# An eighth block by seven products, ordinary units placed by phase, and a weight sum made by an accumulating DMA

## The chip, the core and the metric

The kernel runs on one core of one Trainium2 chip. The metric is the device time of one execution in microseconds (us). The core's engines are named as in the profile: PE (TensorE's matmuls), PEld (its weight loads), DVE (VectorE), ACT (ScalarE), POOL (GpSimd) and SP (SyncE, which only issues DMAs here).

## The reference

Two layers work on x of 256 tokens by 2048 columns, in float32:

```
h  = RMSNorm(x);  z = h @ w_in                    # 2048 x 3584
A  = chunked spatial gating of gelu(z[:, :2048])  # 2 chunks of 128 tokens
B  = sliding-window attention with sinks on the rest of z
x += concat(RMSNorm(A), RMSNorm(B)) @ w_out       # 2048 x 2048
h2 = RMSNorm(x)
x += (silu(h2 @ w_gate) * (h2 @ w_up)) @ w_down   # 2048 x 5632, twice, and 5632 x 2048
```

Three quarters of the matmul work lies in the last line, the feed-forward part (FFN below), and the change is there.

## The kernel before

**Split products.** Each float32 product is made of three matmuls. `split2` makes two tiles of a raw weight tile (128 x 2 x 512): ACT casts it to `wh` (L95) and DVE subtracts to get the rest, `wl` (L96). `mm3` (L125 to L127) multiplies the activation's high part with `wh` and `wl`, and its low part with `wh`. Raw weights come by SP's DMA queue (`raw_load`) into a ring of six tiles, `wh` and `wl` have rings of four.

**Ordinary units.** `unit` takes one raw tile and does 12 matmuls with 512 columns: two halves of the tile, two blocks of 128 tokens, three matmuls each. A block of 512 FFN columns takes 8 units for the gate and 8 for up (`gate_up`, through `even`), then Silu and product (L656, L660). `down` multiplies one or two finished blocks by `w_down`, four column blocks of 512 after one another, and DVE adds each result to the residual `xres` (L680). Both write to a pair of PSUM banks called `dacc` while the other stream is running, and to `acc` afterwards.

**Blocks by seven products.** `seven` treats gate and up weights and the two token blocks as a 2 x 2 by 2 x 2 block product and gets it with 7 products in place of 8. It needs sums of the activations (`ext`, made once per layer in `combine`) and sums of the weights, made by DVE for each block. Its `s_unit` splits one tile and does 6 matmuls. **Phase A** has four products, 16 s_units in four groups: b11 (m0 in the matmuls' tile names), t1 = b11 + b12 (m1), t2 = t1 + b22 (m3) and b12 + b22 (m2). Three weight sums of 128 x 1024 go with each group (L594 to L596). At the middle, ACT and DVE combine the banks into `m1`, `u1`, `c21` and `c22` (L605 to L612). **Phase B** has three products, 12 s_units: b21 (n0), t2 + b21 (n1) and b22 (n2). The fourth sum (L621) is in this phase; the four t2 tiles are kept for it. At the end DVE and ACT make `sg` (L628 to L632), and `act_T` transposes it on PE (`ps_f`) and splits it (L560, L561), as it does after a `gate_up`.

**Order.** The work is written out by a planner. `tick` moves a clock by 1 per ordinary unit and by 0.5 per s_unit, and `later` puts off a step by so many units: `act_T` comes 2 and 3 units after its block. In the FFN the list `S_BLOCKS` is the stream of blocks by seven products, and `STD_ORDER` the other stream: four gate_ups (blocks 0, 2, 4, 6) and the down products of all eleven blocks. After each s_unit the loop at L695 adds 0.5 x `STD_SHARE` to what it owes to the other stream, and emits as many ordinary units as are due; at a turn (the middle and the end of a seven-block) it owes at least 2. The other stream yields False, and emits nothing, while a down waits for the `act_T` of one of its blocks. A scheduler then orders the instructions within a short distance.

The loop before:

```python
for said in s_stream():
    owed = max(owed, 2.0) if said == "turn" else owed + said * STD_SHARE
    while owed >= 1.0 and next(other, False):
        owed -= 1.0
```

Of the kernel before, what the change touches and what calls it, by code (L numbers as in the profile page):

```python
# [12 lines left out]
F32 = mybir.dt.float32  # L13
F32R = mybir.dt.float32r
BF16 = mybir.dt.bfloat16
AF = mybir.ActivationFunctionType
ALU = mybir.AluOpType
# [4 lines left out]
P = 128  # L22
# [4 lines left out]
HD = 64  # L27
NH = 16
NKV = 4
GRP = NH // NKV  # L30
# [5 lines left out]
NB = 512  # L36
# [3 lines left out]
NI = 3584 // NB  # L40
NFF = DFF // NB
ND = D // NB
S_BLOCKS = (1, 3, 5, 7, 8, 9, 10)
STD_ORDER = (
    ("gu", 0), ("gu", 2), ("down", (0, 1)), ("gu", 4), ("down", (2, 3)), ("gu", 6),
    ("down", (4, 5)), ("down", (6, 7)), ("down", (8, 9)), ("down", (10,)),
)
STD_SHARE = 1.42
RL = 512
WARM = 12  # L50

# [12 lines left out]
def trunk(ctx, tc, x, xt, w_in, w_out, w_gate, w_up, w_down, sgu_w, sgu_g, consts,  # L64
          rel_bias, onehot, radd, out):
    nc = tc.nc

    cp = ctx.enter_context(tc.tile_pool(name="cp", bufs=1))
    wp = ctx.enter_context(tc.tile_pool(name="wp", bufs=1))
    tp = ctx.enter_context(tc.tile_pool(name="tp", bufs=8))  # L70
    zp = ctx.enter_context(tc.tile_pool(name="zp", bufs=8))
    ap = ctx.enter_context(tc.tile_pool(name="ap", bufs=2))
# [7 lines left out]
        return t.bitcast(F32)  # L80

    def raw_load(src, parts=1):
        raw = wp.tile([P, 2, NB], F32, tag="raw", name="raw", bufs=6)
        n = 2 // parts
        for i in range(parts):
            nc.sync.dma_start(raw[:, i * n : (i + 1) * n, :], src[:, i * n : (i + 1) * n, :])
        return raw
# [32 lines left out]
    def small_ps(shape, name):  # L120
        pool, tag = ((pm, "sm"), (pd, "dacc"))[next(turns) % 2]
        return pool.tile(shape, F32, tag=tag, name=name)
# [25 lines left out]

    cst = cp.tile([P, L, C_L], F32, tag="cst", name="cst")
    nc.sync.dma_start(cst, consts)  # L150
    junk = cp.tile([P, NB], BF16, tag="junk", name="junk")
    nc.vector.memset(junk, 1.0)
    heat = small_ps([P, NB], "heat")
    for i in range(WARM):
# [8 lines left out]
    def small(shape, name):  # L163
        return sp.tile(shape, F32, tag=name, name=name)
# [27 lines left out]
        return ps  # L192

    def sum_sq(dst, src):
        nc.scalar.activation(junk[:, : src.free_size()], src, AF.Square, accum_out=dst)

    def finish_rms(ss, width):
        tot = small([P, 1], "tot")
# [57 lines left out]
    for lay in range(L):  # L256
# [62 lines left out]
        ob = {}  # L319
# [8 lines left out]
        def attend(g, t, par, zkv=zkv, kT=kT, qT=qT, ob=ob, bias=bias, layer=layer):  # L328
            nk = (t + 1) * P
            k0 = SEQ - nk  # L330
            nh = 2 * len(par)
            heads = [h for h in range(GRP) if h % 2 in par]
            step = heads[1] - heads[0]
            nkb = nk // P
            nsink = layer["nsink"]
            s = ap.tile([P, nh, nk], F32, tag="spt", name="s", bufs=4)
            for r in par:
                ps = small_ps([P, 2, nk], "ps_s")
                for i in range(2):
                    h = g * GRP + 2 * i + r  # L340
                    nc.tensor.matmul(
                        ps[:, i, :],
                        qT[h // 8][HD * r : HD * r + HD, (h % 8) // 2, t * P : (t + 1) * P],
                        kT[HD * r : HD * r + HD, g, :nk],
                        start=True,
                        stop=True,
                    )
                nc.vector.scalar_tensor_tensor(
                    s[:, par.index(r) :: len(par), :], ps, 1.0 / math.sqrt(HD),
                    bias[g][:, r::2, k0:], ALU.mult, ALU.add,  # L350
                )
            m = small([P, nh], f"m{nh}")
            nc.vector.tensor_reduce(m, s, AX.X, ALU.max)
            hs = slice(g * GRP + heads[0], (g + 1) * GRP, step)
            nm = small([P, nh], f"nm{nh}")
            nc.vector.scalar_tensor_tensor(nm, m, -1.0, nsink[:, hs], ALU.mult, ALU.min)
            es = small([P, nh], f"es{nh}")
            nc.vector.tensor_tensor(es, nm, nsink[:, hs], ALU.subtract)
            den = small([P, nh], f"den{nh}")
            for i in range(nh):  # L360
                nc.scalar.activation(
                    s[:, i, :], s[:, i, :], AF.Exp, bias=nm[:, i : i + 1],
                    accum_out=den[:, i : i + 1],
                )
            nc.scalar.activation(es, es, AF.Exp)
            rden = small([P, nh], f"rden{nh}")
            nc.vector.tensor_tensor(rden, den, es, ALU.add)
            nc.vector.reciprocal(rden, rden)
            pt = ap.tile([P, nh * nkb, P], F32, tag="spt", name="pt", bufs=4)

            def turn():
                pst = small_ps([P, nh * nkb, P], "ps_p")
                s4 = s.rearrange("p h (b k) -> p (h b) k", k=P)
                for i in range(nh * nkb):
                    nc.tensor.transpose(pst[:, i, :], s4[:, i, :], ident)
                nc.vector.tensor_copy(pt, pst)

            def weigh():
                pv = small_ps([P, nh, HD], "ps_v")
                for i in range(nh):  # L380
                    for b in range(nkb):
                        nc.tensor.matmul(  # L382
                            pv[:, i, :],
                            pt[:, i * nkb + b, :],
                            zkv[b][:, (NKV + g) * HD : (NKV + g + 1) * HD],
                            start=b == 0,
                            stop=b == nkb - 1,
                        )
                if (g, t) not in ob:
                    ob[g, t] = ap.tile([P, GRP * HD], F32, tag=f"ob{t}", name="ob", bufs=1)  # L390
                o3 = ob[g, t].rearrange("p (h d) -> p h d", d=HD)
                nc.vector.tensor_tensor(o3[:, heads[0] :: step, :], pv, bc(rden, HD), ALU.mult)

            later(3, turn)
            later(5, weigh)
# [172 lines left out]
        def seven(b, lay=lay, pairs2=pairs2, ext2=ext2, act_later=act_later):  # L568
            bank = [pa.tile([P, NB], F32, tag="acc", name=f"m{i}") for i in range(4)]

            def s_unit(raw, m, i, op, first, last):
                wh, wl = split2(raw)
                for j in range(2):
                    ah, al = (op(2 * i + j, h) for h in range(2))
                    mm3(bank[m], ah, al, wh[:, j, :], wl[:, j, :], first and j == 0, last and j == 1)
                tick(0.5)

            def a_op(k, t):
                return lambda p, h: pairs2[p][:, h, k, t * P : (t + 1) * P]

            def e_op(n):
                return lambda p, h: ext2[p][:, h, n, :]

            kept = []
            for i in range(4):
                b12 = raw_load(w_up[lay, b, i, 0])
                b11 = raw_load(w_gate[lay, b, i, 0])
                b22 = raw_load(w_up[lay, b, i, 1])
                t1 = wp.tile([P, 2, NB], F32, tag="raw", name="t1", bufs=6)
                t2 = ap.tile([P, 2, NB], F32, tag="spt", name="t2", bufs=4)  # L590
                first, last = i == 0, i == 3
                s_unit(b11, 0, i, a_op(0, 0), first, last)
                yield 0.5
                nc.vector.tensor_tensor(t1, b11, b12, ALU.add)  # L594
                nc.vector.tensor_tensor(t2, t1, b22, ALU.add)
                nc.vector.tensor_tensor(b12, b12, b22, ALU.add)  # L596
                s_unit(t1, 1, i, e_op(1), first, last)
                yield 0.5
                s_unit(t2, 3, i, e_op(2), first, last)
                yield 0.5  # L600
                s_unit(b12, 2, i, e_op(0), first, last)
                yield 0.5
                kept.append(t2)
            m1 = zp.tile([P, NB], F32, tag="z", name="m1")
            nc.scalar.copy(m1, bank[0])  # L605
# [9 lines left out]
            for i in range(4):  # L615
                b21 = raw_load(w_gate[lay, b, i, 1])
                b22 = raw_load(w_up[lay, b, i, 1])
                first, last = i == 0, i == 3
                s_unit(b21, 0, i, a_op(1, 0), first, last)
                yield 0.5  # L620
                nc.vector.tensor_tensor(kept[i], kept[i], b21, ALU.add)  # L621
                s_unit(kept[i], 1, i, a_op(1, 1), first, last)
                yield 0.5
                s_unit(b22, 2, i, e_op(3), first, last)
                yield 0.5
            sg = [m1, c21]
            for t, m in ((0, m1), (1, c21)):
                nc.vector.tensor_tensor(m, bank[t], m, ALU.add)  # L628
# [9 lines left out]
        def s_stream(seven=seven):  # L638
            for b in S_BLOCKS:
                yield from seven(b)  # L640
# [52 lines left out]
        other = std_stream()  # L693
        owed = 0.0
        for said in s_stream():  # L695
            owed = max(owed, 2.0) if said == "turn" else owed + said * STD_SHARE
            while owed >= 1.0 and next(other, False):
                owed -= 1.0
        seven_done[0] = True
        for went in other:  # L700
            if not went:
# [89 lines left out]
```

## Time and profile before

| | us |
|---|---|
| median of 3 runs (lowest, highest) | 2028.45 (2026.97, 2030.02) |
| profiled execution | 2025.57 |
| its span, first to last instruction | 2023.9 |
| first matmul of a seven-block, layer 0 and layer 1 | 299.9 and 1305.5 |
| last matmul of a seven-block, layer 0 and layer 1 | 986.4 and 1991.1 |
| granted TensorE clock, mean | 0.994 |

In the profile a row names engine, line, operation and tiles as out<-in, with buffer numbers left out. Busy time is the union of an engine's instructions. A matmul's duration is modelled and longer than the distance between two starts, so for PE and for an engine without gaps the starts are what is read. A window row gives busy time and instruction counts of each engine in one stretch, then the granted clock, the share of the 16 DMA engines, and GB/s.

### The profile page before, as it was taken

What the parts mean: (1) busy time and instruction counts of PE and PEld (TensorE: products, weight loads), DVE (VectorE), ACT (ScalarE), POOL (GpSimd) and SP (SyncE); (2) the same over time, 40 slices, a digit from 0 to 9 for tenths busy, and PEclk for the clock granted to TensorE, in tenths of its full rate; (3) what the DMA queues carried; (4) which work ended last, traced back from release to release, by engine and by line L of the source; (5) the groups of instructions that cost most, each with busy time, mean ns of one, the idle gap of its engine ahead of it and who ended that gap; (6) DMA issues with size and microseconds to landing.
All of it is one profiled execution on the core that took longest, in us unless ns stands there. A gap on an engine that the chain in (4) does not pass through costs nothing.

```text
span 2023.9 us, 24694 instructions
## 1 busy us (share of the span) xinstructions
PE 1984.0 (98%) x8990; PEld 1618.5 (80%) x8990; DVE 1666.0 (82%) x1925; ACT 1132.3 (56%) x1415; POOL 67.5 (3%) x65
## 2 busy tenths in 40 slices
PE   8999999999999999999899999999999999999997
PEld 6878888888888888877687788888888888888776
DVE  5767689898989898997867776898989898989976
ACT  6455566555555555554654655666555555555543
POOL 1211000000000000000002100000000000000000
PEclk9999999999999999999999999999999999999999
DMA  9643556565766576665555344565656565657653
GB/s 323 226 162 134 187 178 227 201 235 194 238 209 234 201 236 212 234 204 193 198 188 192 131 156 179 175 233 203 239 206 234 202 239 202 233 204 241 215 186 137
DMA packets 117401, 416.02 MB, mean 206 GB/s; under 512 B 12912, under 2 KB 15088, under 8 KB 117280
## 3 DMA queue, kind: packets, MB, share of 16 engines
q1 hardware_dynamic: 115136, 407.01, 58.4%
q0 software_dynamic: 2144, 7.44, 1.2%
q8 instruction: 70, 1.15, 0.2%
q14 instruction: 51, 0.42, 0.1%
HBM read 412.27 MB, written 4.23 MB: 206 GB/s over the span
## 4 chain that ended last, share of the span: by engine, by line
PE 85%; DVE 9%; issue 2%; DMA 1%; ACT 1%; POOL 1%; SPq 0%; POOLq 0%; ACTq 0%; DVEq 0%
PE dacc L125 12%; PE dacc L126 12%; PE dacc L127 12%; PE acc L126 8%; PE acc L125 8%; PE acc L127 8%; DVE wl L96 4%; PE m L126 4%; PE m L127 4%; PE m L125 4%; PE n L126 3%; PE n L127 3%; PE n L125 3%; PE ps_v L382 1%; DMA raw<-in_w_gate_dram 1%
## 5 line engine op out<-in xcount | busy, mean ns | idle before, releaser
L95 ACT CAST wh<-raw 128x1024 fp32r<-128x1024 f32 (+1 forms) x706 | 739.5, 1050 | 593.2 <-PE dacc L127 293.2
L96 DVE TENSOR_TENSOR wl<-raw,wh 128x1024 fp32r<-128x1024 f32 (+1 forms) x706 | 853.7, 1219 | 207.9 <-ACT wh L95 198.5
L95 ACT CAST wh<-t 128x1024 fp32r<-128x1024 f32 x168 | 177.1, 1054 | 184.6 <-PE dacc L127 116.9
L125 PE MATMUL dacc<-wh,aT 128*128 128x512 f32 x640 | 251.4, 393 | 2.3 <-DVE xres L680 1.5
L127 PE MATMUL dacc<-wh,aT 128*128 128x512 f32 x640 | 250.0, 391 | 0.0
L126 PE MATMUL dacc<-wl,aT 128*128 128x512 f32 x640 | 249.9, 391 | 0.0
L96 DVE TENSOR_TENSOR wl<-t,wh 128x1024 fp32r<-128x1024 f32 x168 | 204.0, 1219 | 17.4 <-ACT wh L95 15.4
L125 PE MATMUL dacc<-wh,hT 128*128 128x512 f32 x512 | 200.3, 391 | 0.3
L126 PE MATMUL dacc<-wl,hT 128*128 128x512 f32 x512 | 199.5, 390 | 0.3 <-DVE wl L96 0.2
L127 PE MATMUL dacc<-wh,hT 128*128 128x512 f32 x512 | 199.4, 389 | 0.0
L126 PE MATMUL acc<-wl,hT 128*128 128x512 f32 x448 | 176.8, 395 | 7.8 <-DVE wl L96 7.8
L125 PE MATMUL acc<-wh,hT 128*128 128x512 f32 x448 | 180.6, 406 | 2.1 <-ACT wh L95 2.1
L127 PE MATMUL acc<-wh,hT 128*128 128x512 f32 x448 | 176.6, 394 | 0.0
L125 PEld LDWEIGHTS dacc<-wh,aT 128*128 128x128 f32 x640 | 120.1, 188 | 30.1 <-issue 3.1
L127 PEld LDWEIGHTS dacc<-wh,aT 128*128 128x128 f32 x640 | 120.7, 189 | 25.6
L126 PEld LDWEIGHTS dacc<-wl,aT 128*128 128x128 f32 x640 | 120.9, 189 | 24.5
L126 PE MATMUL m<-wl,ext 128*128 128x512 f32 x336 | 132.6, 395 | 4.6 <-DVE wl L96 4.6
L125 PE MATMUL m<-wh,ext 128*128 128x512 f32 x336 | 132.7, 395 | 1.1 <-ACT wh L95 1.1
L127 PE MATMUL m<-wh,ext 128*128 128x512 f32 x336 | 132.1, 393 | 0.0
L125 PE MATMUL acc<-wh,aT 128*128 128x512 f32 x320 | 127.8, 399 | 0.7 <-ACT aT L560 0.7
L126 PE MATMUL acc<-wl,aT 128*128 128x512 f32 x320 | 125.3, 392 | 0.0
L127 PE MATMUL acc<-wh,aT 128*128 128x512 f32 x320 | 124.1, 391 | 0.0
(157 smaller groups left out, 2980.7 us busy)
## 6 DMA issues: line engine op xcount, KB each, us to landing
raw<-in_w_up_dram SPq DMA_DIRECT2D x232, 512.0 KB, 4.3
raw<-in_w_gate_dram SPq DMA_DIRECT2D x176, 512.0 KB, 4.1
raw<-in_w_down_dram SPq DMA_DIRECT2D x176, 512.0 KB, 4.1
raw<-in_w_in_dram SPq DMA_DIRECT2D x108, 512.0 KB, 4.2
raw<-in_w_out_dram SPq DMA_DIRECT2D x64, 512.0 KB, 3.2
bias<-rdram POOLq DMA_DIRECT2D x8, 512.0 KB, 5.6
xr<-in_xt_dram SPq DMA_DIRECT2D x8, 256.0 KB, 6.0
raw<-in_w_in_dram SPq DMA_DIRECT2D x8, 256.0 KB, 5.8
```

The source lines that it names most:

```text
L95: nc.scalar.copy(wh[:, j : j + step, :], src)
L96: nc.vector.tensor_tensor(wl[:, j : j + step, :], src, f(wh[:, j : j + step, :]), ALU.subtract)
L125: nc.tensor.matmul(acc, ah, wh, start=first, stop=False)
L126: nc.tensor.matmul(acc, ah, wl, start=False, stop=False)
L127: nc.tensor.matmul(acc, al, wh, start=False, stop=last)
L382: nc.tensor.matmul(pv[:, i, :], pt[:, i * nkb + b, :], zkv[b][:, (NKV + g) * HD : (NKV + g + 1) * HD], start=b == 0, stop=b == nkb - 1,)
```

## The change

- `S_BLOCKS` has eight blocks (3 to 10) in place of seven, and `STD_ORDER` three gate_ups (0, 1, 2). All down products remain.
- After each s_unit of phase A the loop owes 0.575 ordinary units, after one of phase B 0.23, and 2 at each turn. At most one unit is emitted after an s_unit; at a turn two are emitted, whatever is owed.
- The fourth weight sum goes from DVE to a DMA that POOL issues: after t2's s_unit in phase A, the tile of `w_gate` is added in place to t2 by `accum_op`. Phase B then reads t2 as it is. Phase B's own load of b21 remains, for n0.
- In each group of phase A, b11 is loaded first and t1 is made before b11's split; the other two sums stand directly ahead of the s_units that come before their use.
- The raw ring has seven tiles. Room for it comes from `junk`, the Square results and `ob`, which go into the ring `z` of eight, and from softmax scratch tiles that share tags.

```diff
-S_BLOCKS = (1, 3, 5, 7, 8, 9, 10)
+S_BLOCKS = (3, 4, 5, 6, 7, 8, 9, 10)
 STD_ORDER = (
-    ("gu", 0), ("gu", 2), ("down", (0, 1)), ("gu", 4), ("down", (2, 3)), ("gu", 6),
-    ("down", (4, 5)), ("down", (6, 7)), ("down", (8, 9)), ("down", (10,)),
+    ("gu", 0), ("down", (0, 3)), ("gu", 1), ("down", (1, 4)), ("down", (5, 6)), ("gu", 2),
+    ("down", (2, 7)), ("down", (8, 9)), ("down", (10,)),
 )
-STD_SHARE = 1.42
+SHARE_A = 0.575
+SHARE_B = 0.23
+TURN = 2
...
-        raw = wp.tile([P, 2, NB], F32, tag="raw", name="raw", bufs=6)
+        raw = wp.tile([P, 2, NB], F32, tag="raw", name="raw", bufs=7)
...
-    junk = cp.tile([P, NB], BF16, tag="junk", name="junk")
+    junk = zp.tile([P, NB], BF16, tag="z", name="junk")
...
     def sum_sq(dst, src):
-        nc.scalar.activation(junk[:, : src.free_size()], src, AF.Square, accum_out=dst)
+        void = zp.tile([P, NB], BF16, tag="z", name="void")
+        nc.scalar.activation(void[:, : src.free_size()], src, AF.Square, accum_out=dst)
...
-                    ob[g, t] = ap.tile([P, GRP * HD], F32, tag=f"ob{t}", name="ob", bufs=1)
+                    ob[g, t] = zp.tile([P, GRP * HD], F32, tag="z", name="ob")
...
             for i in range(4):
+                b11 = raw_load(w_gate[lay, b, i, 0])
                 b12 = raw_load(w_up[lay, b, i, 0])
-                b11 = raw_load(w_gate[lay, b, i, 0])
                 b22 = raw_load(w_up[lay, b, i, 1])
-                t1 = wp.tile([P, 2, NB], F32, tag="raw", name="t1", bufs=6)
+                t1 = wp.tile([P, 2, NB], F32, tag="raw", name="t1", bufs=7)
                 t2 = ap.tile([P, 2, NB], F32, tag="spt", name="t2", bufs=4)
                 first, last = i == 0, i == 3
+                nc.vector.tensor_tensor(t1, b11, b12, ALU.add)
                 s_unit(b11, 0, i, a_op(0, 0), first, last)
-                yield 0.5
-                nc.vector.tensor_tensor(t1, b11, b12, ALU.add)
+                yield SHARE_A
                 nc.vector.tensor_tensor(t2, t1, b22, ALU.add)
+                s_unit(t1, 1, i, e_op(1), first, last)
+                yield SHARE_A
                 nc.vector.tensor_tensor(b12, b12, b22, ALU.add)
-                s_unit(t1, 1, i, e_op(1), first, last)
-                yield 0.5
                 s_unit(t2, 3, i, e_op(2), first, last)
-                yield 0.5
+                nc.gpsimd.dma_start(t2, w_gate[lay, b, i, 1], accum_op=ALU.add)
+                yield SHARE_A
                 s_unit(b12, 2, i, e_op(0), first, last)
-                yield 0.5
+                yield SHARE_A
...
                 s_unit(b21, 0, i, a_op(1, 0), first, last)
-                yield 0.5
-                nc.vector.tensor_tensor(kept[i], kept[i], b21, ALU.add)
+                yield SHARE_B
                 s_unit(kept[i], 1, i, a_op(1, 1), first, last)
-                yield 0.5
+                yield SHARE_B
                 s_unit(b22, 2, i, e_op(3), first, last)
-                yield 0.5
+                yield SHARE_B
...
         for said in s_stream():
-            owed = max(owed, 2.0) if said == "turn" else owed + said * STD_SHARE
-            while owed >= 1.0 and next(other, False):
-                owed -= 1.0
+            turn = said == "turn"
+            owed += TURN if turn else said
+            for k in range(TURN):
+                if (turn or (k == 0 and owed >= 1.0)) and next(other, False):
+                    owed -= 1.0
```

More of the change, by code (lines that the diff above doesn't have):

```diff
@@ L351, in attend @@
                 )
-            m = small([P, nh], f"m{nh}")
+            m = small([P, GRP], "m")[:, :nh]
             nc.vector.tensor_reduce(m, s, AX.X, ALU.max)
             hs = slice(g * GRP + heads[0], (g + 1) * GRP, step)
-            nm = small([P, nh], f"nm{nh}")
+            nm = small([P, GRP], "nm")[:, :nh]
             nc.vector.scalar_tensor_tensor(nm, m, -1.0, nsink[:, hs], ALU.mult, ALU.min)
-            es = small([P, nh], f"es{nh}")
+            es = small([P, GRP], "es")[:, :nh]
             nc.vector.tensor_tensor(es, nm, nsink[:, hs], ALU.subtract)
-            den = small([P, nh], f"den{nh}")
+            den = small([P, GRP], "den")[:, :nh]
             for i in range(nh):
@@ L365, in attend @@
             nc.scalar.activation(es, es, AF.Exp)
-            rden = small([P, nh], f"rden{nh}")
+            rden = small([P, GRP], "rden")[:, :nh]
             nc.vector.tensor_tensor(rden, den, es, ALU.add)
```

## The prediction, made before the change was run

> **What bounds the kernel now.** I read the page's first two parts, the groups by form, windows over the feed-forward part (FFN), and VectorE's and TensorE's timelines where windows differ. In the page's shares and 40 slices, PE counts as busy nearly always and DVE reaches 8 or 9 tenths in the FFN halves (slices 7 to 20 and 27 to 40):
> ```profile
> PE 1984.0 (98%) x8990; PEld 1618.5 (80%) x8990; DVE 1666.0 (82%) x1925; ACT 1132.3 (56%) x1415; POOL 67.5 (3%) x65
> DVE  5767689898989898997867776898989898989976
> ```
> Windows of layer 0's FFN (columns: PE, PEld, DVE, ACT, POOL busy us and counts, clock, DMA share, GB/s):
> ```profile
> 300.00:860.00 560.00, 559.49 (x2500) 461.19 (x2499) 496.41 (x486) 322.23 (x334) 1.95 (x2) 1.00 0.65 221
> 860.00:1015.00 155.00, 143.35 (x615) 113.71 (x614) 130.78 (x136) 83.72 (x98) 0.00 (x0) 0.98 0.57 198
> ```
> ```profile
> 884.00:907.00 23.00, 17.96 (x71) 13.18 (x70) 22.89 (x24) 12.84 (x15) 0.00 (x0) 0.93 0.55 182
> 907.00:962.00 55.00, 54.25 (x238) 44.04 (x237) 39.07 (x37) 24.72 (x25) 0.00 (x0) 1.00 0.58 206
> 962.00:979.00 17.00, 14.33 (x51) 10.09 (x50) 16.96 (x18) 8.02 (x9) 0.00 (x0) 0.90 0.52 178
> ```
> Up to 860 PE never starves. Then two stretches have DVE full and PE idle, with slack between: DVE is the bound where "seven" units run without ordinary units beside them. The timelines give the unit prices, from start to start. DVE, saturated:
> ```profile
> 897.12 1.21 DVE L96 TENSOR_TENSOR wl<-raw,wh 128x1024 fp32r<-128x1024 f32 x1
> 898.26 1.22 DVE L594 TENSOR_TENSOR t<-raw 128x1024 f32<-128x1024 f32 x1
> 899.39 0.68 DVE L561 TENSOR_TENSOR aT<-ps_f,aT 128x512 fp32r<-128x512 f32 x1
> 899.99 1.22 DVE L595 TENSOR_TENSOR t<-t,raw 128x1024 f32<-128x1024 f32 x1
> 901.13 1.22 DVE L596 TENSOR_TENSOR raw<-raw 128x1024 f32<-128x1024 f32 x1
> ```
> A 1024-wide operation costs DVE 1.14 us and a 512-wide one 0.60 (L632's and L660's 0.743 us kind 0.66). PE, fed and after a gap:
> ```profile
> 985.32 0.39 PE L125 MATMUL n<-wh,ext 128*128 128x512 f32 x1
> 985.54 0.39 PE L126 MATMUL n<-wl,ext 128*128 128x512 f32 x1
> 985.77 0.39 PE L127 MATMUL n<-wh,ext 128*128 128x512 f32 x1
> ```
> ```profile
> 904.13 0.63 PE L127 MATMUL m<-wh,ext 128*128 128x512 f32 x1
> 904.55 0.63 PE L125 MATMUL m<-wh,ext 128*128 128x512 f32 x1
> 904.98 0.63 PE L126 MATMUL m<-wl,ext 128*128 128x512 f32 x1
> ```
> Fed matmuls start every 0.2267 us (median of all), so a seven-unit (6) is 1.36 us of PE and an ordinary unit (12) 2.72. After the gaps they start every 0.43: the granted clock fell to half for 3.4 us, a loss of 1.7.
>
> **Part 1: matmuls removed.** An ordinary gate-and-up block is 16 x 12 = 192 matmuls, one by seven products 28 x 6 = 168. One more block in two layers: 48 fewer, 48 x 0.2267 = 10.9 us, all on PE's path. **-10.9.**
>
> **Part 2: DVE and ACT.** In the built program DVE's 1024-wide operations fall from 1094 to 1086 (24 more splits, 32 fewer sums: the fourth moves to the DMA) and 14 half-width ones come: 8 x 1.14 = 9.1 against 14 x 0.60 = 8.4 us, nothing in total. ACT gets 24 casts of 1.05 us at a share of 56%: hidden. DVE's 126 extra wait-only instructions I put at nothing: the saturated starts above keep 1.14 with such waits between.
>
> What matters is DVE per place. Phase A, per seven-unit: 1 split and 3/4 of a sum = 1.99, plus 0.575 ordinary units at 1.14 + 0.30 (L680, two 0.60 per four units) = 0.83, together 2.82 us; PE 1.36 + 0.575 x 2.72 = 2.92. So 96%; before, with 0.71 ordinary units, it was 3.01 against 3.29, 91%. Adding turn work (9 half-width operations, act_T), A and the two turns come to about 57.5 us of DVE per block against 59 of PE: it fits, by 1.5 us. Phase B (1.14 + 0.23 x 1.44 = 1.47 against 1.99) has 6 us to spare.
>
> **Part 3: the bare tail goes.** Before, 1.42 plus the turns spends all 144 ordinary units that can run before block 10 is ready too early, and much of the last block and a half stands bare. Window 860 to 1015.6 holds 582 512-column matmuls (131.9 us) and 6.1 us of transposes: 17.6 lost; in layer 1 likewise 16.8. The new rates take 16 x 0.575 + 12 x 0.23 + 4 = 15.96 units per block, 127.7 in eight, of the 136 - 8 = 128 available; in the built order ordinary units reach to the end, and the last turn's two (5.44 us) stand before the transposes that waited 2.83 us at 986. I leave 1.5 us per layer: 34.4 - 3. **-31.5.**
>
> **Part 4: new bare places.** gate_up takes 16 units and a block gives 15.96, so each gate_up ends with a block, and the next down waits for act_T of both (2 and 3 units of planner clock). The built order shows it three times per layer: two units, m0, one unit, then m1 m3 m2 m0 m1 m3 (m2) bare. Ledger from the last n2: PE ends the three units and m0 at 10.0 and would start the second m1 at 16.9, m3 at 18.3. DVE: u1 and the two sg products 1.9, three splits 5.3, sum 6.5, act_T 7.1, t2's split 8.2; then gate_up's two products must wait for PE's third unit (10.0; queued behind them are b12's split and all of the next group): 11.3, split 12.5, act_T 13.1, sum, split, sum, split 17.6, sum, act_T, t2's split 20.5. PE is 0.7 and then 1.5 us late; next come act_T, split, four 1024-wide operations and the second ordinary unit's split at 29.1, where PE is about 1.2 late. Sum 3.4. The bounds: nothing, if DVE had run ahead by its four wl buffers, and 7 us, what 884 to 907 lost. With a third of the 1.7 us half clock, since DVE catches up meanwhile, I take 3.9, and 0.6 more for the longer third place: 2 x (3 x 3.9 + 0.6) = **+24.6.**
>
> [...]
>
> **Part 5: FFN start.** The first units come later (0.575 for 0.71) while DVE still makes the last two hT and ext pairs (2.2 us each). Between 0 and 3 us each; 1.5, as sums now lie ahead of that work: **+3.**
>
> **Part 6: the accumulating DMA.** 64 of 512 KB, issued by POOL. Each waits for t2's cast and split; behind it on POOL stand only later ones and, once per layer, rstd2's two `ir`, for which DVE's `nr` waits. Their input comes 2.8 us of DVE work after t2's split, the issue takes 0.8 (bias row): hidden, else 0.8. The sum is read half a block later, over 28 us. What it can cost is DMA time: q1's packets average 164 ns (58.4% of 16 engines, 115136), q0's 181:
> ```profile
> q1 hardware_dynamic: 115136, 407.01, 58.4%
> q0 software_dynamic: 2144, 7.44, 1.2%
> ```
> At 0.65 for 221 GB/s the engines hold about 340. A phase-A group (11.7 us) loads 3 + 2.3 tiles, 8.1 us at 1.52 each; 3.6 are left for one accumulate. No row shows one: as a plain POOL packet it is 1.7 us, as its whole time to landing (bias, 5.6) 5.6. I take 1.7, the nearest: **0**, and keep the upper end as a rival.
>
> [...]
>
> **Small edits.** b11 loads ahead of b12 on SP and t1 now stands before b11's split; in the built orders the DVE work between a raw buffer's release and its next reader has a median of 11.6 us (10.3 before) against landings of 4.1 to 4.3, so order and seventh tile cost nothing, and L621's 16.4 us of waits for loads, which stalled no matmul, merely vanish. ob and the Square scratch in the z ring may wait for a free buffer: ACT has room; 0, within 2 either way. Attention's PE order barely changes.
>
> **Sum.** -10.9 - 31.5 + 24.6 + 3 = about -15 against the profiled execution's 2025.57 us (span 2023.9 and 1.7 around it): 2010.5. The median of the three runs is 2.9 higher, so: **2013 us.**
>
> **Rivals.** (a) DVE's lead covers the bare places: for it, 866 to 884 ran twelve bare n units without a stall; against, phase A's sums double the shortage. Then -39: 1989. Chance 0.12. (b) Slower: DVE runs short in every block's phase A, its in-order waits for PE (1.8 us in the ledger) eating the 1.5 us margin. Decides at 0.9 us more per block over 16; at 3 us, +48 - 15: 2061; at 2, 2045. For it: 96%; against: no stall at 91% until 860. Chance 0.13. (c) Slower: an accumulate holds the engines over 3.6 us; at 4.6, 64 x 1.0 - 15: 2077. Against: a plain load takes 1.5. Chance 0.07. (d) The two new losses cancel the gain without (b) or (c): same, 0.06. (e) Sums or placement not as described: the built order has 64 accumulates and the rates; 0.02.
>
> **Numbers.** The forecast has 0.60, on its own 2000 to 2023. Faster means by over 0.2% (4 us), about what a measurement can tell: 0.60 + 0.12 + 0.02 = 0.74; same 0.06; slower 0.13 + 0.07 = 0.20. Low 1986 holds (a); high 2042 takes in (d) and the mild half of (b).
>
> **What would show it.** Right: 48 fewer matmuls; ordinary units to each layer's end and no 2.8 us gap there; PE gaps of 3 to 5 us only after the three gate_ups, DVE full there. Wrong: PE waiting for wl all through phase A (b); DMA share near 1 and raws landing late (c); no gaps at all (a).

## The result, and the profile after

The changed kernel takes 2008.67 us (median of five runs, 2003.67 to 2013.38) against 2028.45 before: ratio 0.9907, 95% interval [0.9883, 0.993]. It is faster by 0.9%, clear of the noise. The forecast was 2013, range 1986 to 2042, faster. The profiled execution takes 2011.28 us (span 2009.6) against 2025.57, so the traces differ by 14.3 us. Everything below is in those spans.

The page of the changed kernel: busy engines, DVE's 40 slices, DMA queues (packets, MB, share of 16 engines), and the accumulating DMA's issues (KB each, median us to landing):
```profile
PE 1971.9 (98%) x8942; PEld 1610.9 (80%) x8942; DVE 1664.0 (83%) x1931; ACT 1154.1 (57%) x1441; POOL 120.0 (6%) x129
...
DVE  6767689989899897889866776889898998978896
...
q1 hardware_dynamic: 116288, 411.21, 60.1%
q0 software_dynamic: 11360, 41.00, 11.1%
...
t<-in_w_gate_dram POOLq DMA_DIRECT2D x64, 512.0 KB, 7.0
```
PE has 48 instructions fewer, DVE's total is where it was, and q0 (POOL's queue) went from 1.2 to 11.1%.

Windows of layer 0's FFN (PE, PEld, DVE, ACT, POOL busy us and counts, clock, DMA share, GB/s): the stretch that never starved before and the one that did; then the four places where PE now idles, and two short stretches inside them:
```profile
300.00:860.00 560.00, 549.33 (x2426) 449.30 (x2425) 498.80 (x493) 329.74 (x344) 25.94 (x30) 0.99 0.80 248
860.00:1005.00 145.00, 144.62 (x652) 119.24 (x651) 125.53 (x130) 86.83 (x99) 3.41 (x4) 1.00 0.74 235
384.00:408.00 24.00, 22.06 (x98) 16.96 (x98) 23.68 (x24) 13.40 (x15) 1.72 (x3) 1.00 0.88 263
555.00:578.00 23.00, 21.12 (x95) 16.36 (x94) 22.65 (x23) 13.21 (x15) 2.30 (x3) 1.00 0.85 253
760.00:776.00 16.00, 14.10 (x54) 10.68 (x53) 9.48 (x11) 7.84 (x9) 0.03 (x1) 0.89 0.83 279
812.00:834.00 22.00, 18.67 (x75) 13.89 (x74) 20.09 (x20) 11.11 (x14) 1.70 (x2) 0.92 0.85 245
770.60:774.10 3.50, 3.43 (x8) 2.55 (x9) 1.52 (x2) 1.19 (x3) 0.00 (x0) 0.51 0.71 238
828.60:832.10 3.50, 3.50 (x9) 2.74 (x10) 3.33 (x3) 0.00 (x0) 0.00 (x0) 0.52 0.90 303
```
The loss moved. Before, 860 to 1015 had the gaps and 300 to 860 none; now it is the other way round. Of the four places three are the predicted ones behind a gate_up (around 400, 570 and 823), with DVE nearly full. The fourth, around 768, is different: DVE is busy in only 9.48 of 16 us.

The ledger of both layers counts, for each 512-column matmul, the distance to the next start beyond the cadence of 0.2267 us ("lost"):

| | before | after | difference | forecast |
|---|---|---|---|---|
| matmuls removed, 48 x 0.2267 | | | -10.9 | -10.9 |
| lost from 860 (layer 1: 1865) to the layer's end | 34.5 | 2.8 | -31.7 | -31.5 |
| lost at the three places behind a gate_up | 0 | 24.8 | +24.8 | +24.6 |
| lost in the 10 to 20 us after the FFN's start | 0 | 4.3 | +4.3 | +3 |
| lost around 768 and at the same place in layer 1 | 0 | 7.1 | +7.1 | none |
| scattered elsewhere in the FFN up to 860 | 9.1 | 4.9 | -4.2 | none |
| transposes in the FFN, with the waits around them | 25.7 | 21.1 | -4.6 | none |
| outside the FFN | | | +1.1 | none |
| sum | | | -14.1 | -15 |

### The profile page after: what moved, and what is told of

It reads as the page before. It is cut to its first block, busy times and chain, and to the rows that moved or that the text cites. A ratio compares the mean times of both kernels' runs of the same rounds, so it can differ in the third digit from the quotient of the medians.

```text
span 2009.6 us, 24839 instructions
## 1 busy us (share of the span) xinstructions
PE 1971.9 (98%) x8942; PEld 1610.9 (80%) x8942; DVE 1664.0 (83%) x1931; ACT 1154.1 (57%) x1441; POOL 120.0 (6%) x129
## 3 DMA queue, kind: packets, MB, share of 16 engines
q1 hardware_dynamic: 116288, 411.21, 60.1%
q0 software_dynamic: 11360, 41.00, 11.1%
## 4 chain that ended last, share of the span: by engine, by line
PE 83%; DVE 11%; issue 2%; DMA 2%; ACT 1%; POOL 1%; SPq 0%; DVEq 0%; POOLq 0%; ACTq 0%
PE dacc L128 11%; PE dacc L129 11%; PE dacc L127 10%; PE acc L128 8%; PE acc L129 8%; PE acc L127 7%; DVE wl L98 5%; PE m L129 4%; PE m L128 4%; PE m L127 4%; PE n L128 4%; PE n L129 4%; PE n L127 4%; DMA raw<-in_w_up_dram 1%; DVE raw L601 1%
## 5 line engine op out<-in xcount | busy, mean ns | idle before, releaser
L97 ACT CAST wh<-t 128x1024 fp32r<-128x1024 f32 x192 | 202.3, 1054 | 186.9 <-PE dacc L129 109.7
L98 DVE TENSOR_TENSOR wl<-t,wh 128x1024 fp32r<-128x1024 f32 x192 | 233.5, 1222 | 21.5 <-ACT wh L97 16.3
L127 PE MATMUL m<-wh,ext 128*128 128x512 f32 x384 | 153.3, 399 | 3.7 <-ACT wh L97 3.5
L128 PE MATMUL dacc<-wl,hT 128*128 128x512 f32 x384 | 150.5, 392 | 3.3 <-DVE wl L98 3.3
L128 PE MATMUL m<-wl,ext 128*128 128x512 f32 x384 | 150.6, 392 | 0.6 <-DVE wl L98 0.2
L127 PE MATMUL dacc<-wh,hT 128*128 128x512 f32 x384 | 150.7, 392 | 0.1
L129 PE MATMUL dacc<-wh,hT 128*128 128x512 f32 x384 | 150.2, 391 | 0.0
L129 PE MATMUL m<-wh,ext 128*128 128x512 f32 x384 | 150.0, 391 | 0.0
L128 PEld LDWEIGHTS dacc<-wl,aT 128*128 128x128 f32 x640 | 121.0, 189 | 36.1 <-DVE wl L98 11.1
L603 POOL DMA_DIRECT2D t<-in_w_gate_dram x64 | 54.5, 852 | 1387.2 <-DVE wl L98 754.6
```

The lines of the kernel that those rows point to most:

```text
L97: nc.scalar.copy(wh[:, j : j + step, :], src)
L98: nc.vector.tensor_tensor(wl[:, j : j + step, :], src, f(wh[:, j : j + step, :]), ALU.subtract)
L127: nc.tensor.matmul(acc, ah, wh, start=first, stop=False)
L128: nc.tensor.matmul(acc, ah, wl, start=False, stop=False)
L129: nc.tensor.matmul(acc, al, wh, start=False, stop=last)
L603: nc.gpsimd.dma_start(t2, w_gate[lay, b, i, 1], accum_op=ALU.add)
```

## The experiments

Two theories stood open besides the prediction's terms: that the gain is the placing alone and the new order of the down products spends part of it again, and (the rival) that DVE's room or the accumulating DMA decides.

**1. The order, the DMA, the rates: five kernels.** `order_ready` moves gate_ups ahead so that every down finds its blocks finished before the stream reaches it:

```diff
-    ("gu", 0), ("down", (0, 3)), ("gu", 1), ("down", (1, 4)), ("down", (5, 6)), ("gu", 2),
-    ("down", (2, 7)), ("down", (8, 9)), ("down", (10,)),
+    ("gu", 0), ("gu", 1), ("down", (0, 3)), ("down", (1, 4)), ("gu", 2), ("down", (5, 6)),
+    ("down", (2, 7)), ("down", (8, 9)), ("down", (10,)),
```


> The changed kernel with one edit: STD_ORDER runs the second gate_up straight after the first and each down only on blocks that were finished a whole block earlier (gu 0, gu 1, down (0,3), down (1,4), gu 2, down (5,6), down (2,7), down (8,9), down (10,)). Same matmuls, sums, DMAs. Theory (VectorE bound where seven-units run bare behind a gate_up): the built order has no bare place, so the three gaps per layer (3.1, 3.1 and 6.3 us over the steady cadence in the changed kernel's trace, 24.6 in both layers) go: 1984 us, between 1979 and 1990. Rival (the gaps come from the DMA engines, 0.85 busy there because of the accumulates): nothing is taken off them, 2009 plus or minus 4.

Measured: 1975.45 us, ratio to before 0.9738 [0.9719, 0.9756]. Its windows:
```profile
300.00:860.00 560.00, 558.36 (x2499) 461.18 (x2498) 511.19 (x506) 339.55 (x353) 25.94 (x30) 1.00 0.81 253
860.00:990.00 130.00, 130.00 (x590) 107.57 (x589) 114.78 (x120) 78.88 (x92) 3.40 (x4) 1.00 0.76 242
```
PE has 9 us more of work in the same 560, and DVE 12. Lost in the FFN falls from 22.5 and 21.1 us (layer 0, layer 1) to 6.1 and 5.2, that is by 32.3, about the 24.8 behind the gate_ups and the 7.1 around 768. Both are gone with nothing but another order of nine list entries. The time is below the theory's 1984 and its range (1979 to 1990), because the place around 768 was not in the theory's price.

That place, in the changed kernel's timeline (start, us, engine, line, tiles, idle time and its releaser):
```profile
765.32 0.39 PE L129 MATMUL dacc<-wh,hT 128*128 128x512 f32 x1
...
765.75 1.05 ACT L97 CAST wh<-raw 128x1024 fp32r<-128x1024 f32 x1 [1.66 <-PE dacc L129]
...
766.83 1.23 DVE L98 TENSOR_TENSOR wl<-raw,wh 128x1024 fp32r<-128x1024 f32 x1 [1.12 <-ACT wh L97]
...
768.11 0.50 PE L128 MATMUL n<-wl,hT 128*128 128x512 f32 x1 [0.76 <-DVE wl L98]
```
ACT has cast three ordinary tiles ahead of n0's, PE's program has n0 earlier than two of them. ACT waits for a `wh` buffer (a ring of four) until PE ends a dacc unit, casts n0's tile only then, and PE stands although later tiles are ready. It is a wait of order, not of DVE's room. The same happens again 3 us later (n1's tile, 769.58).

`seven_spread` takes seven blocks and the order of before, with the new loop and its rates set for them:

```diff
-S_BLOCKS = (3, 4, 5, 6, 7, 8, 9, 10)
+S_BLOCKS = (1, 3, 5, 7, 8, 9, 10)
...
-    ("gu", 0), ("down", (0, 3)), ("gu", 1), ("down", (1, 4)), ("down", (5, 6)), ("gu", 2),
-    ("down", (2, 7)), ("down", (8, 9)), ("down", (10,)),
+    ("gu", 0), ("gu", 2), ("down", (0, 1)), ("gu", 4), ("down", (2, 3)), ("gu", 6),
+    ("down", (4, 5)), ("down", (6, 7)), ("down", (8, 9)), ("down", (10,)),
...
-SHARE_A = 0.575
-SHARE_B = 0.23
+SHARE_A = 0.71
+SHARE_B = 0.43
```

> The changed kernel with the blocks and order of before (seven blocks by seven products, four gate_ups), and rates of 0.71 and 0.43, which with the turns take 143.6 of the 144 ordinary units that can run before the last block is ready. It has the 48 matmuls more, but neither the bare tail of before nor bare places behind a gate_up. Theory (the tail cost 31.5 us, the eighth block saves 10.9 and its order gives 25 to 30 back): 2028 - 31.5 = 1997, between 1992 and 2003, so faster than the changed kernel. Rival (the gain is the eighth block's and the DMA sum's): 2017 or more.

Measured: 1989.57 us, 0.9814 [0.9797, 0.9832]. The theory's sign held; its range was missed below by 2.4. So the new placing, with the DMA sum, the seventh tile and the new order of loads and sums beside it, is worth 39 us against before; no run has seven blocks and the new placing alone. The eighth block with the order as changed then costs 19 us again (2008.67), and with an order that fits it brings 14 (1975.45): 10.9 for the matmuls and 3.6 for less lost (14.9 us in both layers against 11.3).

`dve_sum` gives the fourth sum back to DVE in phase B and drops the accumulating DMA:

```diff
-                nc.gpsimd.dma_start(t2, w_gate[lay, b, i, 1], accum_op=ALU.add)
...
+                nc.vector.tensor_tensor(kept[i], kept[i], b21, ALU.add)
                 s_unit(kept[i], 1, i, a_op(1, 1), first, last)
```


> The changed kernel with the fourth weight sum back on VectorE, in phase B, from the b21 tile that is loaded there anyway; no accumulating DMA. Adds four 1.14 us operations to each of 16 blocks (73 us of VectorE), takes 64 DMAs away. Theory: phase B has 6 us of VectorE to spare per block, so 4.6 are hidden: 2009, between 2004 and 2018. Rival (VectorE has no room anywhere, the accumulating DMA is what makes eight blocks possible): the 4.6 us per block come out on TensorE, up to +73, at least 2040. Second rival (the accumulates' traffic costs time): faster than 2003.

Measured: 2011.72 us, 0.992 [0.9906, 0.9935], not to be told from the change itself. DVE is busy for 1730.2 us instead of 1664.0, and PE loses its time at the same places (up to 860 it is busy for 548.81 us, in the change for 549.33). The same edit on `order_ready` (`ready_dve`):

> The kernel with the order of finished blocks (1975.5 us) with the fourth weight sum back on VectorE in phase B, no accumulating DMA. Theory (phase B has 6 us of VectorE to spare, 4.6 are added): 1977, between 1972 and 1984. Rival (its VectorE, without bare places, is now busy enough that the sums show): 1990 or more.

Measured: 1976.19 us, 0.9745 [0.9726, 0.9764], as the theory had it. With seven raw tiles the 64 accumulating DMAs are worth nothing that shows, with either order (3.1 and 0.7 us).

`old_rate` keeps eight blocks and the change's own order, and puts back the loop of before, 0.71 after every s_unit and as many units as are owed:

```diff
-SHARE_A = 0.575
-SHARE_B = 0.23
+SHARE_A = 0.71
+SHARE_B = 0.71
...
-            turn = said == "turn"
-            owed += TURN if turn else said
-            for k in range(TURN):
-                if (turn or (k == 0 and owed >= 1.0)) and next(other, False):
-                    owed -= 1.0
+            owed = max(owed, 2.0) if said == "turn" else owed + said
+            while owed >= 1.0 and next(other, False):
+                owed -= 1.0
```

> The changed kernel with the placing rule of before: after each s_unit, in both phases, 0.71 units are owed, at a turn at least 2, all that is due is emitted at once. Eight blocks, order, DMA sum and seven raw tiles stay. Theory (what the ordinary units stand beside decides): the other stream runs ahead of the blocks that its downs need, and in the built order some 60 seven-units of phase A per layer stand bare in place of 20; each leaves VectorE 0.6 us short, and five turns have no cover. About 50 us of gaps per layer against 21.8: 2009 + 60 = 2069, between 2040 and 2110. Rival (eight blocks and the DMA sum give the gain, placing little): 2009 to 2020.

Measured: 2097.03 us, 1.0344 [1.0325, 1.0362], inside the theory's range. One of its stretches without ordinary units:
```profile
600.00:645.00 45.00, 38.85 (x162) 28.72 (x161) 44.97 (x45) 28.48 (x30) 3.41 (x4) 1.00 0.82 245
```
DVE is busy in 44.97 of 45 us and PE's starts thin out: the bound before, now in the middle of a layer as well. Eight blocks stand or fall with the placing.

**2. What an accumulate may cost.** `twice` issues each accumulating DMA twice; the sum in t2 then holds that weight tile twice.

```diff
                 nc.gpsimd.dma_start(t2, w_gate[lay, b, i, 1], accum_op=ALU.add)
+                nc.gpsimd.dma_start(t2, w_gate[lay, b, i, 1], accum_op=ALU.add)
```


> The changed kernel with each accumulating DMA issued twice (t2 gets the tile twice, so one of the seven products is another one; the time is what counts). Theory (DMA engine time decides, and from 3.6 us of accumulate per phase A group on): two of 3.1 us make 8.1 + 6.2 = 14.3 us per group of 11.7, 2.6 over, 64 times, less what seven raw tiles hold back, some 3 us per block: 2009 + 163 - 48 = 2124, between 2060 and 2170. Rival (an accumulate costs only its landing time, which half a block hides): 2009 plus or minus 5.

Measured: 2032.82 us, 1.0026 [1.0011, 1.0042]. Neither the theory nor the rival: 24 us more than the change, not 115. What PE loses in the FFN rises by 22.9 us. The page's queue line, a piece of the chain of waits, and DVE's row behind it:
```profile
q0 software_dynamic: 20576, 74.56, 19.2%
```
```profile
406.55 8.68 DMA raw<-in_w_up_dram
```
```profile
415.32 1.23 DVE L598 TENSOR_TENSOR t<-t,raw 128x1024 f32<-128x1024 f32 x1 [2.39 <-DMA raw<-in_w_up_dram]
```
A raw load takes 8.7 us here and holds the next sum. That is rival (c)'s picture at twice the load, at a fifth of the 115 us that the theory put on it. The theory charged the accumulates to the 11.7 us of their own phase A group. They are read half a block later, so they may run until then: per block about 36 raw tiles of 1.52 and four or eight of 3.1 us, 54.7 + 12.4 or 54.7 + 24.8, stand against some 82 us of PE. Shared out in that way the engines would fill at about 6.8 us per accumulate, an estimate: (82 - 54.7) / 4. Why 24 us are lost at 6.2 no run shows. POOL's timeline has what may be another reason why the double load came cheap:
```profile
406.08 0.86 POOL L604 DMA_DIRECT2D t<-in_w_gate_dram  x1 [7.86 <-DMA t<-in_w_gate_dram]
409.82 0.84 POOL L603 DMA_DIRECT2D t<-in_w_gate_dram  x1 [2.88 <-DVE wl L98]
420.74 0.86 POOL L604 DMA_DIRECT2D t<-in_w_gate_dram  x1 [10.08 <-DMA t<-in_w_gate_dram]
```
The second of a pair (L604) is issued here 10.9 us after the first (409.82 to 420.74), when that one has landed; POOL waits so 58 times for the 64 pairs, 444.3 us in all. So `twice` runs the two of a pair one after the other, and it does not test one accumulate of 6.2 us within a group.

**3. Even or by phase.** `ready_flat` is `order_ready` with one rate:

```diff
-SHARE_A = 0.575
-SHARE_B = 0.23
+SHARE_A = 0.427
+SHARE_B = 0.427
```

> The kernel with the order of finished blocks, with one rate in both phases: 0.427 after each s_unit, the same 12 units per block. Theory (VectorE's margin in phase A decides): phase A and the turns then hold 54.1 us of VectorE against 52.8 of TensorE per block, 1.3 short, with waits up to 3; times 16 is 20 to 48: 2005, between 1988 and 2025. Rival (only VectorE's total per block counts, 75 us of 82, and its lead over TensorE evens it out): 1975 plus or minus 4.

Measured: 1981.14 us, 0.9769 [0.9751, 0.9786]: 5.7 more than `order_ready`, between the two and nearer the rival. So the difference between the phases is worth 6 us of the gain. The rest of what `old_rate` loses comes with its higher rate and with emitting all that is due at once, and these two were not taken apart.

**4. The seventh raw tile.** Four kernels, all with `order_ready`'s order and rates. `ready_six` is `order_ready` with six raw tiles:

```diff
-        raw = wp.tile([P, 2, NB], F32, tag="raw", name="raw", bufs=7)
+        raw = wp.tile([P, 2, NB], F32, tag="raw", name="raw", bufs=6)
...
-                t1 = wp.tile([P, 2, NB], F32, tag="raw", name="t1", bufs=7)
+                t1 = wp.tile([P, 2, NB], F32, tag="raw", name="t1", bufs=6)
```

> The kernel with the order of finished blocks, with six raw tiles in place of seven. Theory of the prediction (the seventh tile costs and brings nothing): 1975 plus or minus 4. Rival (with the accumulates the DMA engines are 0.81 busy, a load lands in 4.7 to 5.0 us, not 4.2, and six tiles leave too little time): some loads come late, 1982 or more.

Measured: 2048.38 us, 1.0102 [1.0081, 1.0122]. One tile is worth 73 us. `six_dve` has these two lines and `dve_sum`'s edit:

> The order and rates of the 1975 us kernel, six raw tiles, and the fourth sum on DVE instead of the accumulating DMAs. With seven tiles this is 1976; with six tiles and the accumulates it was 2048, its ACT waiting 107 us for w_down loads and 67 us for w_gate loads. Theory A (the seventh tile pays for the accumulates: they make the other loads land later, and six tiles then are too few): with them gone six tiles suffice, 1976 to 1985. Theory B (the seventh tile pays for the new order of loads and sums and for the density of the eight blocks): it stays at 2030 to 2050.

`six_oldsums` has six tiles, the DMA, and in phase A the loads and sums in the order of before:

```diff
+                b12 = raw_load(w_up[lay, b, i, 0])
                 b11 = raw_load(w_gate[lay, b, i, 0])
-                b12 = raw_load(w_up[lay, b, i, 0])
...
-                nc.vector.tensor_tensor(t1, b11, b12, ALU.add)
                 s_unit(b11, 0, i, a_op(0, 0), first, last)
                 yield SHARE_A
+                nc.vector.tensor_tensor(t1, b11, b12, ALU.add)
                 nc.vector.tensor_tensor(t2, t1, b22, ALU.add)
+                nc.vector.tensor_tensor(b12, b12, b22, ALU.add)
                 s_unit(t1, 1, i, e_op(1), first, last)
                 yield SHARE_A
-                nc.vector.tensor_tensor(b12, b12, b22, ALU.add)
```


> The order and rates of the 1975 us kernel, six raw tiles, accumulates kept, but in each phase A group the loads and the three sums in the order of the kernel before (b12 first, t1 after b11's split). Theory B1 (the new order of loads and sums holds raw tiles longer): near 1980, 1973 to 1995. Rival (tile order is not it; eight blocks or the accumulates ask for the tile): 2035 to 2055.

`ready_oldsums` has this last edit alone, with seven tiles:

> The order and rates of the 1975 us kernel with all seven raw tiles and the accumulates, and the loads and sums of phase A in the order of the kernel before. The prediction put the reordering at nothing: 1975, within 4. Rival (three sums in a row ahead of t1's unit starve PE for their 3.4 us at each of 64 groups, 0.3 to 0.5 us each that the lead of four tiles does not cover): 1995 to 2010.

Measured:

| order of loads and sums, fourth sum | seven tiles | six tiles |
|---|---|---|
| new, accumulating DMA | 1975.45 | 2048.38 |
| new, DVE | 1976.19 | 1987.83 (0.9814 [0.9795, 0.9833]) |
| of before, accumulating DMA | 1976.60 (0.9754 [0.9735, 0.9773]) | 1994.25 (0.9843 [0.9823, 0.9863]) |

With seven tiles neither the order of loads and sums nor the DMA changes the time. With six, the new order alone costs 12 us, the DMA alone 18, and both together 73. `six_dve` ends 3 us above theory A's range and `six_oldsums` just inside that of theory B1: each is about right for its own kernel, and the price belongs to the pair. The waits of `ready_six`, and then of `order_ready` (us in total, times, longest):
```profile
ACT wh L97 <- DMA raw<-in_w_down_dram: 106.5, 38, 6.3
ACT wh L97 <- DMA raw<-in_w_gate_dram: 66.5, 17, 7.4
```
```profile
ACT wh L97 <- DMA raw<-in_w_gate_dram: 10.0, 11, 2.7
...
ACT wh L97 <- DMA raw<-in_w_down_dram: 4.5, 6, 1.1
```
`ready_six`'s chain of waits, in one of its bad stretches:
```profile
396.70 6.36 DMA raw<-in_w_gate_dram
...
404.12 1.04 ACT wh L97
...
406.37 0.58 DVE raw L601
...
407.42 1.22 DVE wl L98
...
409.69 1.23 DVE wl L98
...
410.93 5.26 DMA raw<-in_w_gate_dram
```
A load, its cast, DVE's work, and directly behind the `wl` at 409.69 the next load: the ring itself is the chain, and 11.6 of its 19.5 us from 396.7 to 416.2 are the two loads. The loads land no slower than with seven tiles (4.8 us median for `w_gate` against 5.0); they start too late. Six tiles with the order of before and DVE's sum were not run, and why the two together cost more than their sum was not taken apart.

**5. A ninth block.** `nine` makes block 2 by seven products too:

```diff
-S_BLOCKS = (3, 4, 5, 6, 7, 8, 9, 10)
+S_BLOCKS = (2, 3, 4, 5, 6, 7, 8, 9, 10)
...
-    ("gu", 0), ("down", (0, 3)), ("gu", 1), ("down", (1, 4)), ("down", (5, 6)), ("gu", 2),
-    ("down", (2, 7)), ("down", (8, 9)), ("down", (10,)),
+    ("gu", 0), ("gu", 1), ("down", (2,)), ("down", (0, 1)), ("down", (3, 4)), ("down", (5, 6)),
+    ("down", (7, 8)), ("down", (9,)), ("down", (10,)),
...
-SHARE_A = 0.575
-SHARE_B = 0.23
+SHARE_A = 0.48
+SHARE_B = 0.055
```

> A ninth block by seven products (block 2), two gate_ups, down products in the order (2), (0,1), (3,4), (5,6), (7,8), (9), (10), rates 0.48 and 0.055. PE saves 10.9 us more. DVE gets per layer 28 splits, 12 sums and 14 half-width operations more and 16 ordinary units of 1.44 us fewer: about +31 us on the 626 of 690 us that it is busy in the feed-forward part of the 1975 us kernel, so 657 of 684, 96%. Theory (DVE's average decides, its lead evens out the rest, as the single rate for both phases cost only 6 us): 1968, 1960 to 1980. Rival (96% on average is more than the rings can even out; each phase A falls behind by 1 to 3 us): 1985 to 2020.

Measured: 1999.17 us, 0.9869 [0.9847, 0.9891], in the rival's range. It loses 23.5 us per layer in the FFN where `order_ready` loses 6.1 and 5.2: +35.7 against -10.9. Windows of `nine` and of `ready_dve`:
```profile
300.00:860.00 560.00, 550.23 (x2435) 447.14 (x2434) 526.93 (x526) 342.14 (x356) 28.53 (x33) 1.00 0.80 254
```
```profile
300.00:860.00 560.00, 558.41 (x2500) 461.35 (x2499) 538.27 (x533) 340.07 (x353) 1.98 (x2) 1.00 0.70 227
```
So it is not DVE's average, as both theories had it: `ready_dve` keeps DVE busier (538 us against 527) and PE 8 us fuller. In the whole program the two keep DVE busy alike (1728.3 us in `nine`, 1726.5 in `ready_dve`). In `nine` the gaps lie scattered, most of 0.3 to 1.4 us; DVE's timeline at the largest of layer 0, in the phase A that follows the turn at 516 to 520:
```profile
545.68 1.28 DVE L683 TENSOR_TENSOR xres<-dacc,xres 128x512 f32<-128x512 f32 x2
546.87 1.21 DVE L598 TENSOR_TENSOR t<-t,raw 128x1024 f32<-128x1024 f32 x1
```
DVE has no pause in its rows from 537.61 on, ACT's cast of t2 waits 1.55 us for that sum, and PE stands for 1.9. The extra work of `nine` falls where DVE is already full, that of `ready_dve` in phase B where it is not. That reading is argued from these rows; no run separates it from the finer mixing of units in `nine`'s order. It is not enough by itself: by the prediction's prices phase A of `nine` takes 1.99 + 0.48 x 1.44 = 2.68 us of DVE for 2.67 of PE, and `ready_flat`, with 2.60 for 2.52, is shorter of DVE there and lost only 6 us. So the cause of `nine`'s loss stays open.

The best version of all is `order_ready`, 1975.45 us.

## Why the prediction was right

**Part 1, right.** 8942 PE instructions for 8990.

**Part 2, right in its total, its margin misread.** DVE's busy time is 1664.0 for 1666.0 us, and phase A starves for DVE nowhere but at the predicted places, so rival (b) did not come. But the margin of 1.5 us per block was no edge: `ready_flat` puts phase A by the prediction's own prices at 1.99 + 0.427 x 1.44 = 2.60 us of DVE for 2.52 of PE, and costs 6 us in all.

**Part 3, right.** 34.5 us lost became 2.8, against 34.4 and 3. The sum left the transposes out; they brought 4.6 more.

**Part 4, right in its total, one term wrong.** The places lie where the built order put them. The ledger's 3.4 us was 3.06 at each of the first two. The half clock, put at 0.5 to each, did not come there: the clock is 1.00 in both windows. It came whole in the third (0.92), which lost 6.3 with it, against 4.5. Together 12.4 per layer for 12.3. Rival (a) is out: PE's gaps are there, and `order_ready` shows what covering them is worth.

**Not in the sum: the place around 768, +7.1.** The step that fell short is the costing of new places only by DVE's ledger, which says nothing where ACT's order and PE's order of the same tiles differ. It was balanced by two gains not counted either (transposes, scattered gaps, -8.8), so the total is closer than its parts, and that closeness is luck.

**Part 5, near.** 4.3 lost for 3.

**Part 6, right in the zero, wrong in the price, its edge not borne out.** q0's share rose by 9.9% of 16 engines: 0.099 x 16 x 2009.6 / 64 is 49.7 us summed over the 16 engines, or 3.1 us of all of them, for each accumulate. A plain load takes q1's 60.1% x 2009.6 over 784 loads of 512 KB, 1.54. So it was 1.7 us in the sum and is 3.1, 2.0 times a plain load. The edge of 3.6 us is not borne out: in `twice` about 6 us per group cost 24, not 166, though as two accumulates one after the other.

**Small edits: right in the zero, short on the tile.** The order of loads and sums and the seventh tile were said to cost nothing, and together they cost nothing (`ready_oldsums`). But what the tile brings was not asked, since the 16.4 us of waits for loads had stalled nothing before. Without it the rest of the change, with `order_ready`'s order, loses 73 us.

**The placing.** The prediction booked the change's gain under its two large terms, -31.5 and +24.6. The runs give both their own cause: the new placing and the small edits earn 39 us without an eighth block, and the order of the down products takes 33 of what eight blocks so placed could have. How much of the 39 the placing earns alone no run shows; with eight blocks, putting the old placing back costs 88 (`old_rate`).

## What to carry to other kernels

When two streams share an engine that is short in one of them, mix them at a fixed rate to the very end (here the 34.5 us lost at the end of layer 0's and layer 1's FFN became 2.8), and then read the order list for each place where a consumer comes directly behind its producer: moving a ready item in front cost nothing here and was worth more than the change (33.2 us against 19.8). Price a buffer in the kernel that uses it: the waits of the kernel before gave a seventh raw tile no worth, and in `order_ready` it is worth 73 us. An operation that a DMA takes over from an engine that has slack at that point, here the fourth sum, brought nothing with seven raw tiles (1975.45 against 1976.19), and with six it cost 61 us (2048.38 against 1987.83).

## What the hardware showed that was not expected

- **The clock halved after gaps of 0.98 to 2.07 us, and their sizes do not tell when.** Before 770.6 PE had idled 0.98 and 1.30 us, within 3.6 us; before 828.6 it was 1.01 and 2.07, within 5.1. Each time the clock was 0.51 or 0.52 for the next 3.5 us. At 394 to 404, gaps of 0.75, 0.37 and 1.35 us, over ten, left it at 1.00. The total of the gaps does not decide either: 0.98 and 1.30 us come again at the same place in layer 1, before 1771.8, and the clock stays at 1.00:
```profile
1771.80:1775.30 3.50, 3.37 (x13) 2.55 (x14) 1.50 (x2) 1.16 (x2) 0.00 (x0) 1.00 0.63 220
```
In the trace's clock records the slow stretches of the two FFNs begin at 770.70, 828.73 and 1828.83 us; each lasts 3.41 us, at 0.50. What decides whether the clock halves is not shown by these runs.
- **An accumulating DMA took 3.1 us of the 16 engines for 512 KB and landed in 7.0**, and the plain FFN loads beside it in 4.6 to 4.7 instead of 4.1 to 4.3 (`dve_sum`, 4.3). The DMA share in the FFN rose from 0.65 to 0.80, and the time is the one without it (`dve_sum`, 0.69).
- **DVE was busy in 538 of 560 us while PE lost 5 to 6 us in a whole layer's FFN** (`ready_dve`). `nine`, at 527, lost 23.5: a high share by itself said little here.
